# Gated MLP of a two-layer trunk: 16 of 22 up pairs as seven block products, and the down projection in six parts between them

## The chip, the cores and the metric

The kernel runs on one core of one Trainium2 chip. A core has a matrix engine (PE, with its weight loads shown apart as PEld), three engines for elementwise work (DVE, ACT and POOL) and SP, on whose queue nearly all transfers are issued. The metric is the device time of one execution in microseconds; less is better. The program lists each engine's instructions, the engine works through its list in that order, and engines wait for each other by semaphores. So the order of the instructions on an engine is part of the program.

## The reference, cut to what matters

The program computes a decoder trunk of two layers on 512 tokens of width 1024. A layer has a mixer (retention and mLSTM in layer 0, sparse attention in layer 1), a gated MLP with a causal convolution of width 3, and a gated per-layer embedding `e`. The change lies in the MLP and in where `e` is kept:

```
def conv_ffn(h, w_up, conv_w, conv_b, w_down):
    a, b = jnp.split(h @ w_up, 2, axis=-1)
    a = causal_dwconv(a, conv_w, conv_b)
    return (jax.nn.gelu(a) * b) @ w_down
...
        h = h + conv_ffn(rms_norm(h, ffn_norm_g[i]), ffn_w_up[i], ffn_conv_w[i], ffn_conv_b[i], ffn_w_down[i])
        e = rms_norm(p[i] @ ple_w[i], ple_norm_g[i])
        gate = jax.nn.sigmoid(rms_norm(h, ple_gate_norm_g[i]) @ ple_w_gate[i])
```

`w_up` has 2 x 2816 columns and `w_down` 2816 rows, all in float32. A matrix product is made as three products of reduced precision: each operand is split into a rounded high part and a low part (the rest), and high x high, low x high and high x low are summed.

## The kernel before, in words

Activations lie transposed: 128 features on the partitions and the 512 tokens along a row, so that the residual `h` is eight tiles of 128 x 512 (`hp`). The 2816 hidden columns are 22 blocks of 128, numbered f. For each f there is an **up pair**: `mm_up` multiplies the weight columns of the a half and of the b half with the eight normalized activation tiles, 8 x 3 matmuls of 128 x 512 each (`ws`, `mm3`, L162 to L164), into a bank each of PSUM. Both weight tiles come by one DMA of 512 KB each into a `wr` tile; ACT rounds it to the high part `wh` (L134) and DVE subtracts to get the low part `wl` (L135); three sets of these tiles take turns.

`act_up` then makes the hidden block. DVE multiplies the a product by the norm's factor `n.b` (L1326), ACT and two DVE instructions make the convolution (L1329 to L1331), ACT the gelu (L1332), POOL multiplies by `n.b` (L1333), DVE multiplies by the b product (L1334), and the result is split into `gh` (ACT) and `gl` (DVE).

The **down projection** runs in three parts of eight, eight and six f. When the last f of a part is done, `down` goes through the eight output blocks m: one weight tile, 24 or 18 matmuls of 128 x 512, and an addition to `h` by DVE (L1348). A part is one unbroken stretch of PE.

Between the up pairs the embedding `e` of this layer is normed: its squares are summed on ACT and POOL (L218, L220), and POOL multiplies its eight tiles by the norm's factor (L1413). In layer 0 `e` stays in SBUF; in layer 1 it is written to DRAM (tile `emb`) and read back when the MLP begins.

Instructions are issued in the order of the code, except that loads and splits of weights are given a higher priority, so that they move ahead of other work on their engines by up to 500 steps. A tile name is a pool with a fixed number of buffers (`sc`: six scratch tiles, `wr`: three), and an instruction that needs a fresh buffer waits until the last reader of the old one is done.

Of the kernel before, what the change touches and what calls it, by code (L numbers as in the profile page):

```python
# [11 lines left out]
F32 = mybir.dt.float32  # L12
# [15 lines left out]
PARTS = ((0, 8), (8, 16), (16, 22))  # L28
# [13 lines left out]
AHEAD = 500  # L42

# [13 lines left out]
class Norm:  # L57
    def __init__(self):
        self.h, self.l = [], []


class Trunk:
# [83 lines left out]
    def load(self, src, n=1024, cuts=1):  # L146
        nc = self.nc
# [12 lines left out]
    def mm3(self, out, ah, al, bh, bl, first, last):  # L160
        mm = self.nc.tensor.matmul
        mm(out, ah, bh, start=first, stop=False)  # L162
        mm(out, ah, bl, start=False, stop=False)  # L163
        mm(out, al, bh, start=False, stop=last)  # L164
# [46 lines left out]
    def acc_square(self, n, k, src):  # L211
# [4 lines left out]
        else:  # L216
            sq = self.sc()
            nc.scalar.activation(sq, src, AF.Square)  # L218
            eng = nc.vector if k == KD - 1 else nc.gpsimd
            eng.tensor_tensor(n.acc, n.acc, sq, ALU.add)  # L220
# [92 lines left out]
    def ab_mixer(self):  # L313
        nc, I, tc = self.nc, self.I, self.tc
        with ExitStack() as ctx:
# [997 lines left out]
    def ffn(self, i, e):  # L1313
        nc, I, tc = self.nc, self.I, self.tc
        with ExitStack() as ctx:
            fp = ctx.enter_context(tc.tile_pool(name=f"ffn{i}", bufs=1))
            n = self.norm_in(C_FFN + 8 * i)
# [6 lines left out]
            def act_up(f, pa, pb):  # L1324
                a = fp.tile([P, T], F32, name=self.nm("a"), tag="a", bufs=3)
                nc.vector.tensor_tensor(a, pa, n.b, ALU.mult)  # L1326
                c = self.sc()
                cw = C_FCW + 3 * NF * i + 3 * f
                nc.scalar.activation(c, a, AF.Identity, scale=self.col(cw + 2), bias=self.col(C_FCB + NF * i + f))  # L1329
                nc.vector.scalar_tensor_tensor(c[:, 1:], a[:, 0 : T - 1], self.col(cw + 1), c[:, 1:], ALU.mult, ALU.add)  # L1330
                nc.vector.scalar_tensor_tensor(c[:, 2:], a[:, 0 : T - 2], self.col(cw), c[:, 2:], ALU.mult, ALU.add)  # L1331
                nc.scalar.activation(c, c, AF.Gelu_apprx_tanh)  # L1332
                nc.gpsimd.tensor_tensor(c, c, n.b, ALU.mult)  # L1333
                nc.vector.tensor_tensor(c, pb, c, ALU.mult)  # L1334
                hi = fp.tile([P, T], F32R, name=self.nm("gh"), tag="g", bufs=22)
                lo = fp.tile([P, T], F32R, name=self.nm("gl"), tag="g", bufs=22)
                self.split(hi, lo, c)
                gt[f] = (hi, lo)

            def down(part):  # L1340
                f0, f1 = PARTS[part]
                for m in range(KD):
                    hi, lo = self.load(I["w_down"][i, m, :, f0 * P : f1 * P], (f1 - f0) * P)
                    ps = self.bank()
                    for f in range(f0, f1):
                        s = slice((f - f0) * P, (f - f0 + 1) * P)
                        self.mm3(ps, hi[:, s], lo[:, s], gt[f][0], gt[f][1], f == f0, f == f1 - 1)
                    nc.vector.tensor_tensor(self.h[m], self.h[m], ps, ALU.add)  # L1348
# [203 lines left out]
```

## Time and profile before

| | |
|---|---|
| time, median of 3 runs | 1362.65 us (1362.35 to 1362.84) |
| span of the profiled execution | 1361.3 us |
| its granted TensorE clock | 0.999 |
| busy: PE / DVE / ACT / POOL | 1350.9 / 831.5 / 631.1 / 393.3 us |
| share of the span | 99% / 61% / 46% / 29% |

The span goes from the first to the last instruction of one execution; the median of the timed runs lies 1.35 us above it. PE's records overlap, since matmuls are pipelined: the distance from start to start tells the cost of one, not the record's length. The same holds in small for DVE, whose records overlap the next one's start by under 0.1 us when nothing holds them up.

### The profile page before, as it was taken

To read this page: it belongs to the slowest core of one execution; us is meant where nothing else is said; L and a number is where in the kernel's file an instruction comes from. 1 tells how busy PE (TensorE), PEld (TensorE's weight loads), DVE (VectorE), ACT (ScalarE), POOL (GpSimd) and SP (SyncE) were. 2 spreads that over 40 slices of the span, in tenths; PEclk is the share of its full clock that TensorE was granted. 3 is DMA by queue.
4 is the path that set the end of the run, shared out by engine and by line. 5 is a ranking of instruction groups with operands and counts; after the bars stand their busy time and mean duration, and the time that the engine had idled before them with its cause. 6 is when DMAs were issued, how large, how long until landed. Compare 5 with 4: busy or idle time off the path is not lost.

```text
span 1361.3 us, 17932 instructions
## 1 busy us (share of the span) xinstructions
PE 1350.9 (99%) x6702; PEld 1119.9 (82%) x6702; DVE 831.5 (61%) x1296; ACT 631.1 (46%) x1087; POOL 393.3 (29%) x388
## 2 busy tenths in 40 slices
PE   9999999999999999999999999999999999999998
PEld 7888888888888888888788888888888888888887
DVE  6765866565356534557777878766665346435555
ACT  5357526444224313345366888674544133323432
POOL 3356422122032101130421887672122031101120
PEclk9999999999999999999999999999999999999999
DMA  6533333333333332233253221111433333332232
GB/s 221 157 100 93 109 93 108 93 93 102 100 93 93 93 103 96 75 119 121 82 157 117 82 71 52 32 52 54 167 96 105 93 94 95 103 96 89 82 113 74
DMA packets 44096, 135.05 MB, mean 99 GB/s; under 512 B 5348, under 2 KB 5988, under 8 KB 44008
## 3 DMA queue, kind: packets, MB, share of 16 engines
q1 hardware_dynamic: 43720, 133.76, 31.9%
q8 instruction: 53, 0.87, 0.3%
q14 instruction: 35, 0.29, 0.1%
q10 hardware_dynamic: 288, 0.14, 0.0%
HBM read 124.69 MB, written 5.25 MB: 95 GB/s over the span
## 4 chain that ended last, share of the span: by engine, by line
PE 96%; DVE 1%; ACT 1%; POOL 1%; issue 0%; POOLq 0%; ACTq 0%
PE ps L162 28%; PE ps L163 27%; PE ps L164 27%; PE ps L1068 3%; PE ps L1043 2%; PE ps L1012 2%; PE ps L1013 1%; PE ps L392 1%; PE ps L1014 1%; POOL acc L220 1%; PE ps L938 1%; PE ps L961 0%; PE ps L257 0%; PE ps L249 0%; PE ps L460 0%; DVE xf L806 0%
## 5 line engine op out<-in xcount | busy, mean ns | idle before, releaser
L162 PE MATMUL ps<-y,wh 128*128 128x512 f32 (+1 forms) x1112 | 433.1, 391 | 0.9 <-ACT y L134 0.9
L134 ACT ACTIVATE wh<-wr 128x1024 fp32r<-128x1024 f32 (+2 forms) x216 | 223.3, 1036 | 449.4 <-PE ps L163 367.8
L163 PE MATMUL ps<-y,wh 128*128 128x512 f32 (+1 forms) x1112 | 430.8, 388 | 0.0
L164 PE MATMUL ps<-y,wl 128*128 128x512 f32 (+1 forms) x1112 | 429.1, 388 | 0.0
L135 DVE TENSOR_TENSOR wl<-wr,wh 128x1024 fp32r<-128x1024 f32 (+2 forms) x199 | 246.8, 1241 | 93.6 <-ACT wh L134 92.3
L162 PEld LDWEIGHTS ps<-y,wh 128*128 128x128 f32 x1112 | 209.4, 188 | 44.5 <-ACT y L134 1.3
L164 PEld LDWEIGHTS ps<-y,wl 128*128 128x128 f32 x1112 | 208.8, 188 | 42.9
L163 PEld LDWEIGHTS ps<-y,wh 128*128 128x128 f32 x1112 | 209.1, 188 | 41.9
L1333 POOL TENSOR_TENSOR sc<-sc,rb 128x512 f32<-128x512 f32 x44 | 58.8, 1337 | 469.1 <-ACT sc L1332 469.1
L220 POOL TENSOR_TENSOR acc<-acc,sc 128x512 f32<-128x512 f32 x48 | 74.9, 1561 | 238.3 <-ACT sc L218 235.1
L162 PE MATMUL ps<-gh,wh 128*128 128x512 f32 x352 | 136.9, 389 | 0.0
L163 PE MATMUL ps<-gl,wh 128*128 128x512 f32 x352 | 136.6, 389 | 0.0
L164 PE MATMUL ps<-gh,wl 128*128 128x512 f32 x352 | 136.3, 389 | 0.0
L1348 DVE TENSOR_TENSOR hp<-hp,ps 128x512 f32<-128x512 f32 x48 | 33.0, 687 | 128.7 <-PE ps L164 128.7
L1028 POOL TENSOR_SCALAR pr<-pr,sm,gate 128x512 f32<-128x512 f32 (+3 forms) x128 | 76.4, 610 | 29.5 <-DVE sm L1026 24.9
L1326 DVE TENSOR_TENSOR a<-ps,rb 128x512 f32<-128x512 f32 x44 | 30.3, 689 | 84.5 <-PE ps L164 84.5
L163 PEld LDWEIGHTS ps<-gl,wh 128*128 128x128 f32 x352 | 66.1, 188 | 13.7
L162 PEld LDWEIGHTS ps<-gh,wh 128*128 128x128 f32 x352 | 66.1, 188 | 13.7
L164 PEld LDWEIGHTS ps<-gh,wl 128*128 128x128 f32 x352 | 66.1, 188 | 13.7
L1017 ACT ACTIVATE pr<-ps,nmx 128x512 f32<-128x512 f32 (+3 forms) x128 | 68.2, 543 | 14.7 <-DVE nmx L1015 10.2
L1334 DVE TENSOR_TENSOR sc<-ps,sc 128x512 f32<-128x512 f32 x44 | 30.3, 688 | 68.9 <-POOL sc L1333 64.1
L1332 ACT ACTIVATE sc<-sc 128x512 f32<-128x512 f32 x44 | 27.8, 632 | 85.5 <-DVE sc L1331 85.3
(300 smaller groups left out, 2013.6 us busy)
## 6 DMA issues: line engine op xcount, KB each, us to landing
wr<-in_w_up_dram SPq DMA_DIRECT2D x88, 512.0 KB, 3.5
wr<-in_w_down_dram SPq DMA_DIRECT2D x32, 512.0 KB, 3.5
wr<-in_w_plg_dram SPq DMA_DIRECT2D x16, 512.0 KB, 3.6
wr<-in_w_down_dram SPq DMA_DIRECT2D x16, 384.0 KB, 3.1
hp<-in_xT_dram SPq DMA_DIRECT2D x16, 256.0 KB, 4.6
wr<-in_w_abo_dram SPq DMA_DIRECT2D x8, 512.0 KB, 3.7
wr<-in_w_dram SPq DMA_DIRECT2D x8, 512.0 KB, 3.6
wr<-in_w_q_dram SPq DMA_DIRECT2D x8, 512.0 KB, 3.6
```

The costliest lines, as they stand in the source:

```text
L134: self.nc.scalar.activation(hi, src, AF.Copy)
L135: (eng or self.nc.vector).tensor_tensor(lo, src, hi.bitcast(F32), ALU.subtract)
L162: mm(out, ah, bh, start=first, stop=False)
L163: mm(out, ah, bl, start=False, stop=False)
L164: mm(out, al, bh, start=False, stop=last)
L220: eng.tensor_tensor(n.acc, n.acc, sq, ALU.add)
L1017: nc.scalar.activation(pr[:, b], s[:, b], AF.Exp, bias=nmx[:, b : b + 1], accum_out=sm[:, bs[b] : bs[b] + 1])
L1028: nc.gpsimd.tensor_scalar(prs[b], prs[b], sm[:, b : b + 1], gate[:, j, hd, 1 + b : 2 + b], ALU.mult, ALU.mult)
L1068: nc.tensor.matmul(po[0:m, cols], vv[i][:, b, g, 0:m], src, start=False, stop=last and b == 1 and i == 0 and part == 0)
L1326: nc.vector.tensor_tensor(a, pa, n.b, ALU.mult)
L1333: nc.gpsimd.tensor_tensor(c, c, n.b, ALU.mult)
L1348: nc.vector.tensor_tensor(self.h[m], self.h[m], ps, ALU.add)
```

## The change

**Up pairs.** The first six pairs of a layer (`PLAIN = 6`) stay as they were. Pairs 6 to 21 are made as a 2 x 2 x 2 block product with seven instead of eight block products. The blocks are the halves of the 1024 features (four tiles each), the halves of the tokens (256 each) and the two weight columns a and b. A block product is 4 x 3 matmuls of 128 x 256, so a pair is 84 matmuls of 256 columns where it was 48 of 512. Three PSUM banks hold the sums; ACT copies partial sums out of PSUM between products, and DVE adds them.

**Sums of the activations.** `forms`, called after pair 1, makes the sums and differences of activation blocks that the seven products need, with `n.b` folded in: four rounds, each of four DVE instructions of 512 columns that scale or split, two more splits whose low part is left to POOL, and four of 256 on DVE.

**Sums of the weights.** For each of these pairs DVE makes four additions of 512 columns (in `load`, `open` and `rest`) and the low parts of three 1024-wide and one 512-wide tile. `load` brings both weight tiles of a pair.

**Down projection.** Six parts of three or four f. Each part is four jobs of two output blocks m; one job is put after each up pair as soon as its part is complete, and five jobs are left after the last pair. DVE adds to `h` 48 times a layer instead of 24.

**Embedding.** `e` is written to DRAM in both layers, read once for its squares, with the sums on DVE (`early`), and read again after the last pair (`back`); POOL's multiplication by its norm moves into the gate stage (`scaled`).

```diff
-PARTS = ((0, 8), (8, 16), (16, 22))
+PARTS = ((0, 3), (3, 7), (7, 11), (11, 15), (15, 19), (19, 22))
+PLAIN = 6
+H = T // 2
...
+    def forms(self, n, c0):
+        nc = self.nc
+        minus = self.sc()
+        nc.scalar.activation(minus, n.b, AF.Copy, scale=-1.0)
+        sub = lambda out, a, b: nc.vector.tensor_tensor(out, a, b, ALU.subtract)
+        neither = lambda out, a, b: nc.vector.scalar_tensor_tensor(out, a, -1.0, b, ALU.mult, ALU.subtract)
+        n.f = []
+        for k in range(KD // 2):
+            x1, x2 = self.sc(), self.sc()
+            for x, kk in ((x1, k), (x2, k + KD // 2)):
+                nc.vector.scalar_tensor_tensor(x, self.h[kk], self.col(c0 + kk), minus, ALU.mult, ALU.mult)
+            ta, tb = self.sc(), self.sc()
+            b11, b12, b21, b22 = x1[:, :H], x1[:, H:], x2[:, :H], x2[:, H:]
+            sub(ta[:, :H], b11, b12)
+            neither(ta[:, H:], b22, ta[:, :H])
+            sub(tb[:, :H], b22, b12)
+            neither(tb[:, H:], b21, ta[:, H:])
+            one = self.y()
+            self.split(one[:, :H], one[:, H:], b11, nc.gpsimd)
+            got = {1: (one[:, :H], one[:, H:])}
+            for src, left, right in ((x2, 2, 3), (ta, 5, 6), (tb, 7, 4)):
+                hi, lo = self.y(), self.y()
+                self.split(hi, lo, src, nc.gpsimd if left == 2 else nc.vector)
+                got[left], got[right] = (hi[:, :H], lo[:, :H]), (hi[:, H:], lo[:, H:])
+            n.f.append(got)
...
+                def load(me):
+                    f = me.f
+                    me.one = self.wp.tile([P, 1024], F32, name=self.nm("wr"), tag="wr")
+                    me.two = self.slot(f % 4).rearrange("p a t -> p (a t)")
+                    nc.sync.dma_start(me.one, I["w_up"][i, f])
+                    me.s3 = fp.tile([P, T], F32, name=self.nm("es"), tag="es", bufs=2)
+                    nc.sync.dma_start(me.two, I["w_up"][i, NF + f])
+                    nc.vector.tensor_tensor(me.s3, me.one[:, :T], me.two[:, :T], ALU.add)
+                    nc.vector.tensor_tensor(me.two[:, :T], me.two[:, :T], me.two[:, T:], ALU.add)
+
+                def open(me):
+                    me.halves((1, 2), me.one, self.wp, ("wh", "wl"))
+                    nc.vector.tensor_tensor(me.one[:, :T], me.one[:, :T], me.two[:, :T], ALU.add)
+
+                def rest(me):
+                    nc.vector.tensor_tensor(me.one[:, T:], me.one[:, T:], me.one[:, :T], ALU.add)
+                    me.halves((5, 4), me.two, fp, ("fh", "fl"))
+                    me.w[7] = [fp.tile([P, T], F32R, name=self.nm(t), tag=t) for t in ("eh", "el")]
+                    self.split(*me.w[7], me.s3)
+                    me.halves((6, 3), me.one, fp, ("gh", "gl"))
...
+            def product(ps, w, name, first):
+                hi, lo = w[name]
+                for k in range(KD // 2):
+                    s = slice(k * P, k * P + P)
+                    self.mm3(ps, hi[:, s], lo[:, s], *n.f[k][name], first and k == 0, k == KD // 2 - 1, skip_group_check=True)
+
+            def up(f):
+                w = weights(f)
+                one, two, three = [self.ps(t)[:, :H] for t in "aab"]
+                sa, sb = self.sc(), self.sc()
+                copy = lambda out, ps: nc.scalar.activation(out, ps, AF.Copy)
+                a = a_tile()
+                product(one, w, 1, True)
+                copy(sa[:, :H], one)
+                product(two, w, 2, True)
+                nc.vector.tensor_tensor(a[:, :H], two, sa[:, :H], ALU.add)
+                product(one, w, 6, False)
+                copy(sa[:, H:], one)
+                product(three, w, 5, True)
+                copy(sb[:, :H], three)
+                product(one, w, 7, False)
+                copy(sb[:, H:], one)
+                product(three, w, 3, False)
+                nc.vector.tensor_tensor(a[:, H:], three, sa[:, H:], ALU.add)
+                product(one, w, 4, False)
+                nc.vector.tensor_tensor(sb[:, H:], sb[:, H:], sb[:, :H], ALU.add)
+                c = conv(f, a, True)
+                nc.vector.tensor_tensor(c[:, :H], c[:, :H], one, ALU.mult)
+                nc.vector.tensor_tensor(c[:, H:], c[:, H:], sb[:, H:], ALU.mult)
+                keep(f, c)
...
+                if f == 1:
+                    self.forms(n, C_FFN + 8 * i)
+                if jobs:
+                    down(*jobs.pop(0))
+                e.early(f - 1)
+                for part, (f0, f1) in enumerate(PARTS):
+                    if f == f1 - 1:
+                        jobs += [(part, j) for j in range(KD // 2)]
```

The instructions themselves, at three places. A row holds the line of its own kernel, the operation, output and inputs, and the shape; a number after a name tells one tile from another.

**Where `forms` begins.** DVE in layer 0's MLP, from pair 0's last multiplication on, first before and then in the changed kernel. `a`, `sc` and `g` are the tiles of `act_up`, `hp` is `h`, `cols` holds the columns of gains and taps.

```order
L1334 TENSOR_TENSOR sc_2286<-ps_2232,sc_2286 128x512
L1330 SCALAR_TENSOR_TENSOR sc_2361<-a_2359,cols,sc_2361 128x511
L1331 SCALAR_TENSOR_TENSOR sc_2361<-a_2359,cols,sc_2361 128x510
L135 TENSOR_TENSOR gl_2294<-sc_2286,gh_2293 128x512
L1326 TENSOR_TENSOR a_2436<-ps_2380,rb_2277 128x512
L135 TENSOR_TENSOR wl_2485<-wr_2483,wh_2484 128x1024
L1334 TENSOR_TENSOR sc_2361<-ps_2334,sc_2361 128x512
L1330 SCALAR_TENSOR_TENSOR sc_2438<-a_2436,cols,sc_2438 128x511
```

```order
L1389 TENSOR_TENSOR sc_2295<-ps_2241,sc_2295 128x512
L1375 SCALAR_TENSOR_TENSOR sc_2370<-a_2368,cols,sc_2370 128x511
L265 SCALAR_TENSOR_TENSOR sc_2383<-hp_1684,cols,sc_2381 128x512
L265 SCALAR_TENSOR_TENSOR sc_2384<-hp_1687,cols,sc_2381 128x512
L1376 SCALAR_TENSOR_TENSOR sc_2370<-a_2368,cols,sc_2370 128x510
L137 TENSOR_TENSOR g_2303<-sc_2295,g_2302 128x512
L259 TENSOR_TENSOR sc_2387<-sc_2383 128x256
L1386 TENSOR_TENSOR a_2549<-ps_2493,rb_2286 128x512
L137 TENSOR_TENSOR wl_2600<-wr_2598,wh_2599 128x1024
L259 TENSOR_TENSOR sc_2388<-sc_2384,sc_2383 128x256
L260 SCALAR_TENSOR_TENSOR sc_2387<-sc_2384,sc_2387 128x256
L265 SCALAR_TENSOR_TENSOR sc_2408<-hp_1684,cols,sc_2381 128x512
```

Before, pair 2's convolution (on `a_2436`) comes six rows after pair 1's. Now the rows of `forms` (L259, L260, L265) stand behind pair 1's, and the convolution of pair 2 (on `a_2549`) comes 43 rows after pair 1's.

**The first additions to `h`.** DVE in the changed kernel at the end of that stretch. `sc_2551` is pair 2's hidden block, `sc_2631` pair 3's and `sc_2740` pair 4's; `hp_1684` is output block 0.

```order
L1389 TENSOR_TENSOR sc_2551<-ps_2524,sc_2551 128x512
L1376 SCALAR_TENSOR_TENSOR sc_2631<-a_2629,cols,sc_2631 128x510
L137 TENSOR_TENSOR wl_2793<-wr_2785,wh_2792 128x1024
L234 TENSOR_TENSOR acc_2485<-acc_2485,sc_2782 128x512
L1376 SCALAR_TENSOR_TENSOR sc_2740<-a_2738,cols,sc_2740 128x510
L137 TENSOR_TENSOR g_2559<-sc_2551,g_2558 128x512
L1414 TENSOR_TENSOR wr_2785<-wr_2785,ep_2786 128x512
L1389 TENSOR_TENSOR sc_2631<-ps_2604,sc_2631 128x512
L1417 TENSOR_TENSOR wr_2785<-wr_2785 128x512
L1478 TENSOR_TENSOR hp_1684<-hp_1684,ps_2649 128x512
```

Pair 2's low part `g_2559`, on which the first down jobs' last matmuls wait, now stands 60 rows behind pair 1's first convolution instruction, and the first addition to `h` (L1478) 64 rows behind it. Before, no addition to `h` stands in this stretch.

**One stage with a block product pair and a down job.** DVE in the changed kernel, from the low part of a down job's weights to the next pair's multiplications, and PE at the end of a second product and the start of a fifth.

```order
L137 TENSOR_TENSOR wl_4421<-wr_4419,wh_4420 128x1024
L1459 TENSOR_TENSOR a_4148<-ps_4145,sc_4146 128x256
L137 TENSOR_TENSOR gl_4303<-wr_4118,gh_4302 128x1024
L1375 SCALAR_TENSOR_TENSOR sc_4240<-a_4148,cols,sc_4240 128x511
L1451 TENSOR_TENSOR a_4316<-ps_4312,sc_4314 128x256
L1409 TENSOR_TENSOR es_4457<-wr_4454,ep_4455 128x512
L137 TENSOR_TENSOR fl_4295<-ep_4119,fh_4294 128x1024
L1376 SCALAR_TENSOR_TENSOR sc_4240<-a_4148,cols,sc_4240 128x510
L1410 TENSOR_TENSOR ep_4455<-ep_4455 128x512
L137 TENSOR_TENSOR wl_4475<-wr_4454,wh_4474 128x1024
L1463 TENSOR_TENSOR sc_4240<-sc_4240,ps_4143 128x256
L1464 TENSOR_TENSOR sc_4240<-sc_4240,sc_4147 128x256
```

```order
L176 MATMUL ps_2932<-y_2471,wh_2792 128x256
L177 MATMUL ps_2932<-y_2472,wh_2792 128x256
L178 MATMUL ps_2932<-y_2471,wl_2793 128x256
L176 MATMUL ps_2933<-y_2400,fh_2914 128x256
L177 MATMUL ps_2933<-y_2401,fh_2914 128x256
L178 MATMUL ps_2933<-y_2400,fl_2915 128x256
```

The load of the tile `wr_4454` (a later pair's a weights, read by L1409) goes into the buffer that `wr_4419` of the down job gives free, so it is issued after the first row is done. A plain pair has seven DVE instructions (two `wl`, L1386, two of the convolution, L1389, one low part); a block product pair with its job has 19. PE now changes its weights after each 256 columns instead of 512.

More of the change, by code (lines that the diff above doesn't have):

```diff
@@ new lines, in ffn, with weights @@
+            ahead = [Weights(PLAIN)]
+            def weights(f):
+                with tc.high_priority(offset=AHEAD):
+                    now = ahead.pop()
+                    if f + 1 < NF:
+                        ahead.append(Weights(f + 1))
+                        ahead[0].load()
+                    now.rest()
+                    if ahead:
+                        ahead[0].open()
+                return now.w
+            def product(ps, w, name, first):
[3 more added lines that the diff above has]
+                    self.mm3(ps, hi[:, s], lo[:, s], *n.f[k][name], first and k == 0, k == KD // 2 - 1, skip_group_check=True)
@@ L1344, in down @@
+            def down(part, j):
+                f0, f1 = PARTS[part]
+                w = (f1 - f0) * P
+                hi, lo = self.load_parts([I["w_down"][i, m, :, f0 * P : f1 * P] for m in (2 * j, 2 * j + 1)], w)
+                self.cycle = ("b",)
+                for b in range(2):
+                    m = 2 * j + b
                     ps = self.bank()
                     for f in range(f0, f1):
[L1346 removed]
+                        s = slice(b * w + (f - f0) * P, b * w + (f - f0 + 1) * P)
@@ L1361, in ffn @@
-            down(part)
+                if f < PLAIN:
+                    if f == PLAIN - 1:
+                        with tc.high_priority(offset=AHEAD):
+                            ahead[0].load()
+                            ahead[0].open()
+                    act_up(f, *mm_up(f))
+                else:
+                    up(f)
+                if f == 1:
[3 more added lines that the diff above has]
+                e.early(f - 1)
@@ L1362, in ffn, with __init__ @@
+                for part, (f0, f1) in enumerate(PARTS):
+                    if f == f1 - 1:
+                        jobs += [(part, j) for j in range(KD // 2)]
+            e.back()
+            for job in jobs:
+                down(*job)
             self.cycle = ("a",)
     class Embed:
-        def __init__(self, trunk, i, place, away=None):
+        def __init__(self, trunk, i, place, away):
             self.k, self.i, self.place, self.away = trunk, i, place, away
```

116 lines of the change are left out of this document (67 added, 49 removed).

## The prediction

> **What bounds the kernel now.** I read the page's shares first, then the chain of waits, then the matrix engine's start times.
>
> ```profile
> span 1361.3 us, 17932 instructions
> PE 1350.9 (99%) x6702; PEld 1119.9 (82%) x6702; DVE 831.5 (61%) x1296; ACT 631.1 (46%) x1087; POOL 393.3 (29%) x388
> PE 96%; DVE 1%; ACT 1%; POOL 1%; issue 0%; POOLq 0%; ACTq 0%
> DVE hp L1348 <- PE ps L164: 128.7, 46, 5.0
> ```
>
> PE is busy for all but 10 us, and 96% of the chain that ended last is PE. DVE's additions to `h` wait for PE, not the other way. So PE time taken away is gained in full, as long as no other engine becomes late; and any wait that PE gets is lost in full. The change does both kinds of thing: fewer columns through PE, more work on DVE.
>
> **Term 1: the products.** A pair was 48 matmuls of 512 columns and becomes 84 of 256, for 16 pairs in each of two layers. The last stretch of the run holds both widths with nothing between them:
>
> ```profile
> 1334.82 0.39 PE L163 MATMUL ps<-y,wh 128*128 128x512 f32 x1
> ...
> 1350.68 0.39 PE L164 MATMUL ps<-y,wl 128*128 128x512 f32 x1
> 1350.91 0.28 PE L162 MATMUL ps<-y,wh 128*128 128x256 f32 x1
> ...
> 1356.54 0.28 PE L164 MATMUL ps<-y,wl 128*128 128x256 f32 x1
> ```
>
> From the first to the second row are 70 steps: 15.86 / 70 = 0.2266 us for 512 columns. From the third to the fourth are 47: 5.63 / 47 = 0.1198 us for 256, which is 53% and not half. Each of these has its own weight load in both cases. A pair goes from 48 x 0.2266 = 10.88 us to 84 x 0.1198 = 10.06 us, so seven products instead of eight save not an eighth but 7.5%: 0.81 us. Over 32 pairs: **-26.0 us**. If 256 columns cost just half (0.1133 us), it would be 32 x 1.36 = 43.5 us; that is the upper bound.
>
> The Trainium skill, "TensorE: Matmul & The Clock Gate", section "Back-to-back issue gap", lists 518 cycles for 512 columns and 262 for 256; by that ratio (0.506) term 1 would be an estimated 40 us. The trace's 0.1198 us disagrees, and I take the trace.
>
> **Term 2: a stage in which a block product pair meets a down job.** PE needs 10.06 us and 24 matmuls of 512, 5.44 us: 15.5 us. DVE's 19 instructions there, by start to start:
>
> ```profile
> 1160.16 1.22 DVE L135 TENSOR_TENSOR wl<-wr,wh 128x1024 fp32r<-128x1024 f32 x1
> 1161.30 0.68 DVE L135 TENSOR_TENSOR gl<-sc,gh 128x512 fp32r<-128x512 f32 x1
> ...
> 227.88 0.75 DVE L231 SCALAR_TENSOR_TENSOR y<-hp,cols,y 128x512 fp32r<-128x512 f32 x1
> 228.55 0.68 DVE L306 TENSOR_TENSOR hp<-hp,ps 128x512 f32<-128x512 f32 x1
> ...
> 264.13 0.73 DVE L1330 SCALAR_TENSOR_TENSOR sc<-a,cols,sc 128x511 f32<-128x511 f32 x1
> 264.90 0.75 DVE L1331 SCALAR_TENSOR_TENSOR sc<-a,cols,sc 128x510 f32<-128x510 f32 x1
> 265.57 0.68 DVE L135 TENSOR_TENSOR gl<-sc,gh 128x512 fp32r<-128x512 f32 x1
> 266.18 0.68 DVE L1326 TENSOR_TENSOR a<-ps,rb 128x512 f32<-128x512 f32 x1
> L1295 DVE TENSOR_TENSOR pt<-ps,pt 128x256 fp32r<-128x256 f32 x16 | 6.7, 419 | 4.3 <-ACT pt L1046 4.3
> wr<-in_w_up_dram SPq DMA_DIRECT2D x88, 512.0 KB, 3.5
> y<-emb SPq DMA_DIRECT2D x8, 256.0 KB, 5.0
> L134 ACT ACTIVATE wh<-wr 128x1024 fp32r<-128x1024 f32 x196 | 207.2, 1059 | 415.0 <-PE ps L163 344.1 <-issue 32.9 <-PE ps L164 19.8
> L1329 ACT ACTIVATE sc<-a,cols 128x512 f32<-128x512 f32 x44 | 35.5, 808 | 4.2 <-DVE a L1326 3.9
> L1332 ACT ACTIVATE sc<-sc 128x512 f32<-128x512 f32 x44 | 27.8, 632 | 85.5 <-DVE sc L1331 85.3
> L1046 ACT ACTIVATE pt<-ps 128x256 fp32r<-128x256 f32 x16 | 6.5, 408 | 4.5 <-PE ps L1043 4.5
> ```
>
> 1024 columns take 1.14 us, a scalar-tensor-tensor of 512 0.67, one of the convolution 0.77, a plain 512 0.61 (I use 0.62). For 256 there is only a record of 0.419; as the 512 record stands 0.07 above its step, I use 0.38. The stage: 4 x 1.14 + 8 x 0.62 + 5 x 0.38 + 2 x 0.77 = 13.0 us, 84% of 15.5. DVE also closes a loop there with a transfer: the low part of the down weights frees the buffer, the next weights land 3.5 us later, and L1409 behind it waits for them. From that low part to L1409 the loop takes 3.7 us with its signals; then 15 instructions, L1409 the first, run until the next such low part is done: 10.4 us by the steps above. That makes 14.1 us, 1.4 under PE. So I cost the stage at **0**, covered by PE. The loop's upper end: records (10.4 becomes 11.2) and a transfer as slow as `emb`'s 5.0 us give 16.4 us, 0.9 us over PE.
>
> The jobs with three f in a part bring PE's share to 14.1 us, level with the loop. In the stages up to f = 9 the squares of `e` and one norm cost DVE some 3 us more in all; the 16% it has free takes them. The 48 additions to `h` are among the 19. ACT has four copies of 256, four splits of 1024, the convolution's start, the gelu and two splits of 512: 4 x 0.41 + 4 x 1.06 + 0.81 + 3 x 0.63 = 8.6 us of 15.5. The transfers of `e` (8 more writes in layer 0, 16 reads a layer) are short beside the weights on SP's queue, and POOL's multiplications in the gate stage (8 of 1.34 us by L1333's row below) lie beside PE's 8 x 24 matmuls of 5.4 us: all at 0; uncovered they would be 8 x 1.34 = 10.7 us a layer.
>
> **Term 3: the stretch from `forms` to the first additions to `h`.** Here I find no cover. DVE stands in line 64 instructions deep between pair 1's first convolution and the first addition to `h`, and PE's last matmuls of the first down jobs wait for `g_2559` and then, for their bank, for that addition. The 64: 5 of 1024 (5.7 us), 2 of 768 (0.88 by the record below less 0.07: 1.8), 8 scale instructions of `forms` (8 x 0.67 = 5.4), 16 of 256 (16 x 0.38 = 6.1), 8 of the convolution (8 x 0.77 = 6.2), 25 of 512 (25 x 0.62 = 15.5): 40.6 us.
>
> ```profile
> L135 DVE TENSOR_TENSOR wl<-wr,wh 128x768 fp32r<-128x768 f32 x16 | 15.3, 955 | 0.1
> 259.88 0.69 DVE L1326 TENSOR_TENSOR a<-ps,rb 128x512 f32<-128x512 f32 x1 [0.73 <-PE ps L164]
> ```
>
> The clock of this starts when PE ends pair 1's a product, just before 259.88; pair 1's first convolution instruction began at 264.13, 4.25 us later, and nothing ahead of it changes. So the first addition to `h` ends at 4.25 + 40.6 + 0.7 = 45.6 us. PE has until then pairs 2, 3 and 4 and 27 matmuls of down jobs: 171 x 0.2266 = 38.8 us. DVE is late by **6.8 us in each layer**, if nothing slows it down.
>
> But POOL works in this stretch too, and then DVE is slowed:
>
> ```profile
> 289.10 0.74 DVE L1330 SCALAR_TENSOR_TENSOR sc<-a,cols,sc 128x511 f32<-128x511 f32 x1
> 289.29 1.69 POOL L220 TENSOR_TENSOR acc<-acc,sc 128x512 f32<-128x512 f32 x1 [6.54 <-ACT sc L218]
> 289.88 1.66 DVE L1331 SCALAR_TENSOR_TENSOR sc<-a,cols,sc 128x510 f32<-128x510 f32 x1
> L1331 DVE SCALAR_TENSOR_TENSOR sc<-a,cols,sc 128x510 f32<-128x510 f32 x44 | 43.9, 997 | 1.4
> L1326 DVE TENSOR_TENSOR a<-ps,rb 128x512 f32<-128x512 f32 x44 | 30.3, 689 | 84.5 <-PE ps L164 84.5
> L1333 POOL TENSOR_TENSOR sc<-sc,rb 128x512 f32<-128x512 f32 x44 | 58.8, 1337 | 469.1 <-ACT sc L1332 469.1
> L931 POOL TENSOR_TENSOR y<-ep,y 128x256 fp32r<-128x256 f32 x8 | 5.6, 733 | 0.0
> ```
>
> L1331 takes 0.75 us alone and 1.66 beside POOL's addition: 0.91 us lost, and its mean over the kernel is 997 ns. L1326, which reads one operand from PSUM, has a mean of 689 and never shows it. Before, this cost nothing, as DVE had 39% to spare; in this stretch it has nothing. POOL's instructions there are the low parts of `forms` (4 of 512, 4 of 256) and three multiplications by `n.b`: 7 x 0.95 + 4 x 0.45 (733 ns less the same 0.3 us of overlap) = 8.4 us, of which a tenth falls on PSUM readers: 7.6 us. The range: 0, if POOL's work falls into DVE's waits, to the whole of POOL's time, 7 x 1.34 + 4 x 0.73 = 12.3. I take 7.6, since the queue leaves DVE hardly a wait. Together 6.8 + 7.6 = 14.4 us a layer; layer 1 has the same order. Term 3: **+28.8 us**, from 13.6 to 38.
>
> The Trainium skill, "SBUF — State Buffer", section "Who interferes with whom", says that a DVE instruction with two SBUF inputs and a POOL instruction that reads SBUF exclude each other; the rows above agree, and by it all of POOL's 12.3 us would stand against DVE, 38 us for term 3.
>
> **Sum.** 1361.3 - 26.0 + 0 + 28.8 = 1364.1 us of span, and 1.35 more for the median of runs (1362.65 against 1361.3): **1365.5 us**. The saving and the new stall cancel; a stall of 13.0 us a layer is where they do.
>
> **Rivals.**
>
> *The stall is small.* POOL's instructions hit DVE's waits, or DVE gets ahead of my list: 6.8 us a layer, 1361.3 - 26.0 + 13.6 + 1.35 = 1350.3 us. For it: several of the rows in the stretch wait for ACT, so DVE has holes that POOL may use. Against: 1.66 us rows come even where DVE is half idle. Chance 0.22.
>
> *The stages run at DVE's pace.* Place: the loop of down weights, transfer and L1409. Price: at 16.4 us instead of 15.5, 0.9 us on each of some 28 stages, 25 us: 1390 us, slower. It decides from 1.4 us of delay in the loop on. For it: 3.5 us is a median with one or two transfers at a time, and in-order DVE rows wait on ACT, which waits on PE. Against: the pair's other weights have a buffer of their own and land a stage ahead, and DVE is only 84% full. Chance 0.15.
>
> *256 columns cost half.* The array streams half the columns in half of 0.2266 us, and the end of the run is slowed by something else: 43.5 us saved, with the stall 1348 us. The 47 even steps speak against it; 0.05. The table of the Trainium skill cited above would have it nearly so.
>
> *The change does not do what it says.* The order shows 84 matmuls of 256 in each such pair, so only a clock below 0.999 could undo it; 0.03, about 1375 us.
>
> **How the numbers follow.** My forecast, stall of 11 to 18 us a layer and stages at PE's pace, has 0.55: by itself 1359 to 1373 us. A measurement of this kernel tells 0.2% (2.7 us) from no change: faster ends at 1359.9, slower begins at 1365.4. Of my 0.55, 0.05 is faster, 0.23 the same and 0.27 slower. With the rivals: faster 0.05 + 0.22 + 0.05 = 0.32, same 0.23, slower 0.27 + 0.15 + 0.03 = 0.45. The range for 8 in 10 goes from 1347 (small stall, a little less than its 6.8 us) to 1382 (a third to a half of the loop's price on top of the forecast).
>
> **What would show it.** Term 1: starts 0.12 us apart in the 256-column rows, 10.1 us a pair. Term 2: PE without gaps from f = 7 on, 15.5 us from job to job, and L1409 with a wait of about 1 us for its transfer. Term 3: one gap of PE in each layer, ahead of the first matmuls that read `g_2559` and the bank of the first L1478, of 14 us in all, with DVE over 95% busy for 50 us before it, and DVE rows of 1.6 us beside POOL's. The prediction is wrong if PE's idle time in that stretch is under 10 us a layer or if gaps recur in each stage.

## The result, and the profile after

The changed kernel takes **1376.7 us** (median of 4 runs, 1375.1 to 1377.2) against 1362.6 us before, run beside it: ratio 1.0101, 95% interval 1.0089 to 1.0113. It is slower by 1.0%. The forecast was 1365.5 us, the range 1347 to 1382; slower by over 0.2% had the largest chance, 0.45.

The page of the profiled execution, its shares and its chain of waits:

```profile
span 1375.3 us, 20999 instructions
PE 1338.8 (97%) x7854; PEld 1157.2 (84%) x7854; DVE 1054.0 (77%) x1708; ACT 736.0 (54%) x1313; POOL 365.3 (27%) x360
PE 85%; DVE 8%; ACT 3%; issue 2%; POOL 1%; DMA 1%; DVEq 0%; POOLq 0%; ACTq 0%
PEclk9999999989999999999999999999989999999999
```

PE is busy 12 us less than before, but the span is 14 us longer: PE's idle time grew from 10.4 to 36.5 us. The chain, 96% PE before, now has 8% DVE and 3% ACT in it. And the clock row has an 8 in slice 9 and slice 30, the MLP of layer 0 and of layer 1.

The stretch of `forms` on PE, in the timeline of the changed kernel (start, length, and in brackets the idle time and what ended it):

```profile
285.31 0.50 PE L178 MATMUL ps<-g,wl 128*128 128x512 f32 x1 [0.52 <-DVE wl L137]
...
295.64 0.39 PE L178 MATMUL ps<-g,wl 128*128 128x512 f32 x1
298.62 0.47 PE L176 MATMUL ps<-g,wh 128*128 128x512 f32 x1 [2.59 <-ACT sc L1374]
298.93 0.40 PE L177 MATMUL ps<-g,wh 128*128 128x512 f32 x1
300.60 0.50 PE L178 MATMUL ps<-g,wl 128*128 128x512 f32 x1 [1.27 <-DVE wl L137]
...
305.42 1.65 PE L176 MATMUL ps<-g,wh 128*128 128x512 f32 x3 [3.13 <-ACT g L136]
309.43 0.80 PE L177 MATMUL ps<-g,wh 128*128 128x512 f32 x1 [2.36 <-DVE g L137]
310.02 0.63 PE L178 MATMUL ps<-g,wl 128*128 128x512 f32 x1
310.45 0.63 PE L177 MATMUL ps<-g,wh 128*128 128x512 f32 x1
...
314.62 0.44 PE L178 MATMUL ps<-g,wl 128*128 128x512 f32 x1
...
321.50 0.28 PE L176 MATMUL ps<-y,wh 128*128 128x256 f32 x1
```

The five waits add up to 9.9 us. The last is where the prediction put it, ahead of the low part of pair 2's hidden block (`g`, 309.43); the others are for what stands ahead of it in DVE's and ACT's lists. The matmuls between and behind them start up to 0.43 us apart instead of 0.227. The prediction's second condition, the first addition to `h`, is in the row of PE's weight loads:

```profile
312.32 0.29 PEld L176 LDWEIGHTS ps<-g,wh 128*128 128x128 f32 x1 [0.69 <-DVE hp L1478]
```

So up to 312.32 us it is still DVE that sets the pace, also of the slow matmuls. What DVE and POOL do meanwhile:

```profile
282.94 2.31 DVE L137 TENSOR_TENSOR wl<-wr,wh 128x1024 fp32r<-128x1024 f32 x1
289.23 5.96 POOL L137 TENSOR_TENSOR y<-sc,y 128x256 fp32r<-128x256 f32 x2 [5.06 <-ACT y L136]
293.97 0.72 ACT L1374 ACTIVATE sc<-a,cols 128x512 f32<-128x512 f32 x1 [3.39 <-POOL y L137]
294.73 1.01 DVE L1375 SCALAR_TENSOR_TENSOR sc<-a,cols,sc 128x511 f32<-128x511 f32 x1 [1.39 <-ACT sc L1374]
```

DVE's split of 1024 columns, 1.14 us by itself, takes 2.31 us beside POOL; two low parts on POOL take 5.96 us; ACT waits 3.39 us for them before it can start pair 2's convolution, since they hold the scratch tile that it needs, and DVE then waits 1.39 us for ACT.

The clock, from the view of the changed kernel by windows (stretch, length, then busy time of PE, PEld, DVE, ACT and POOL with the number of instructions, the granted clock, DMA share and GB/s):

```profile
300.00:302.00 2.00, 1.40 (x4) 0.82 (x4) 2.00 (x2) 2.00 (x3) 1.69 (x1) 0.77 0.20 30
304.00:306.00 2.00, 0.58 (x1) 0.50 (x2) 2.00 (x4) 1.59 (x3) 0.00 (x0) 0.50 0.04 14
312.00:314.00 2.00, 2.00 (x5) 1.39 (x5) 2.00 (x4) 1.11 (x2) 0.00 (x0) 0.50 0.20 80
316.00:318.00 2.00, 2.00 (x10) 1.64 (x10) 2.00 (x3) 0.62 (x1) 0.00 (x0) 1.00 0.78 259
```

The clock is granted at half from 301.1 to 314.7 us. PE is fully busy from 310 on, and the window from 312 still shows only five matmuls, where the one from 316 shows ten.

Behind the stretch PE is gapless for long (140 us from 420 to 560 without idle time), but not everywhere. At pair 9:

```profile
375.33 0.33 SPq L1406 DMA_DIRECT2D wr<-in_w_up_dram  x1
375.71 0.42 SPq L1549 DMA_DIRECT2D sc<-emb  x1
379.23 1.06 ACT L136 ACTIVATE wh<-wr 128x1024 fp32r<-128x1024 f32 x1 [0.28 <-DMA wr<-in_w_up_dram]
379.96 0.28 PE L177 MATMUL ps<-y,fh 128*128 128x256 f32 x1
380.19 0.71 ACT L1374 ACTIVATE sc<-a,cols 128x512 f32<-128x512 f32 x1
380.80 1.04 ACT L136 ACTIVATE fh<-ep 128x1024 fp32r<-128x1024 f32 x1
381.89 0.39 PE L176 MATMUL ps<-y,fh 128*128 128x256 f32 x1 [1.53 <-ACT fh L136]
```

The next pair's weights land 3.9 us after their issue, a load of `e` for its squares beside them. ACT's rounding of these weights (`wh`) stands in its queue ahead of the convolution and of `fh`, which PE is waiting for. ACT itself waits for the transfer only 0.28 us here. And `fh` has one buffer, which PE's last product of the old pair reads until the row at 379.96: ACT could not have begun the new `fh` before about 380.25, so at most 0.55 us of the 1.53 are due to ACT's queue, and the rest is the rounding itself, which PE has nothing else to cover with.

### The profile page after: what moved, and what is told of

Read it like the earlier page. It is cut to its first block, busy times and chain, and to the rows that moved or that the text cites. A ratio compares the mean times of both kernels' runs of the same rounds, so it can differ in the third digit from the quotient of the medians.

```text
span 1375.3 us, 20999 instructions
## 1 busy us (share of the span) xinstructions
PE 1338.8 (97%) x7854; PEld 1157.2 (84%) x7854; DVE 1054.0 (77%) x1708; ACT 736.0 (54%) x1313; POOL 365.3 (27%) x360
## 4 chain that ended last, share of the span: by engine, by line
PE 85%; DVE 8%; ACT 3%; issue 2%; POOL 1%; DMA 1%; DVEq 0%; POOLq 0%; ACTq 0%
PE ps L176 24%; PE ps L177 24%; PE ps L178 23%; PE ps L1108 3%; PE ps L1083 2%; DVE wl L137 2%; PE ps L1052 1%; PE ps L1053 1%; ACT wh L136 1%; POOL y L137 1%; PE ps L432 1%; DVE sc L1376 1%; PE ps L1054 1%; POOL acc L234 1%; DMA wr<-in_w_up_dram 1%
## 5 line engine op out<-in xcount | busy, mean ns | idle before, releaser
L176 PE MATMUL ps<-y,wh 128*128 128x512 f32 (+1 forms) x664 | 230.9, 351 | 0.9 <-ACT y L136 0.9
L177 PE MATMUL ps<-y,wh 128*128 128x512 f32 (+1 forms) x664 | 229.2, 347 | 0.0
L178 PE MATMUL ps<-y,wl 128*128 128x512 f32 (+1 forms) x664 | 228.0, 346 | 0.0
L176 PE MATMUL ps<-g,wh 128*128 128x512 f32 x544 | 214.3, 398 | 11.3 <-ACT g L136 6.1
L177 PE MATMUL ps<-g,wh 128*128 128x512 f32 x544 | 215.2, 396 | 4.7 <-DVE g L137 4.7
L178 PE MATMUL ps<-g,wl 128*128 128x512 f32 x544 | 214.7, 395 | 3.6 <-DVE wl L137 3.6
L176 PEld LDWEIGHTS ps<-y,wh 128*128 128x128 f32 x664 | 126.0, 190 | 19.0 <-ACT y L136 1.3
L177 PEld LDWEIGHTS ps<-y,wh 128*128 128x128 f32 x664 | 125.8, 189 | 16.0
L178 PEld LDWEIGHTS ps<-y,wl 128*128 128x128 f32 x664 | 125.6, 189 | 15.7
L176 PEld LDWEIGHTS ps<-g,wh 128*128 128x128 f32 x544 | 103.2, 191 | 34.1 <-ACT g L136 7.5
L178 PEld LDWEIGHTS ps<-g,wl 128*128 128x128 f32 x544 | 104.0, 191 | 26.6 <-DVE wl L137 5.3
L177 PEld LDWEIGHTS ps<-g,wh 128*128 128x128 f32 x544 | 103.9, 191 | 25.2 <-DVE g L137 6.2
L176 PE MATMUL ps<-y,fh 128*128 128x256 f32 x256 | 73.0, 285 | 5.0 <-ACT fh L136 5.0
L1478 DVE TENSOR_TENSOR hp<-hp,ps 128x512 f32<-128x512 f32 x96 | 65.0, 680 | 16.7 <-PE ps L178 16.5
L178 PE MATMUL ps<-y,gl 128*128 128x256 f32 x256 | 72.5, 283 | 0.0
```

The source lines that it names most:

```text
L176: mm(out, ah, bh, start=first, stop=False, **kw)
L177: mm(out, ah, bl, start=False, stop=False, **kw)
L178: mm(out, al, bh, start=False, stop=last, **kw)
```

## The experiments

All times are medians; "before" was run again beside each group of runs (1362.2 to 1362.7 us). The changed kernel of 1376.7 us is what each is held against.

### Three quarters of forms left out (x1)

```diff
         for k in range(KD // 2):
+            if k:
+                n.f.append(n.f[0])
+                continue
             x1, x2 = self.sc(), self.sc()
```

> Leaves out three of the four rounds of forms (the sums of round 0 stand in for all; every matmul and every other instruction stays). Theory A (PE's loss of 15.0 us a layer in the forms stretch is DVE's queue there, 64 instructions plus what POOL adds): DVE has 12.3 us less to do by its own instructions and about 4 us less beside POOL, so the stall all but goes: 1376.7 - 2 x 15 = 1347 us, 1343 to 1352. Theory B (the stall hangs on where the first down jobs stand, not on how much DVE does ahead of them): 1370 us or more. Theory C (the stages at DVE's pace cost most of it): at most 10 us less, 1367 us or more.

**1348.6 us**, ratio to before 0.9898 (0.9883 to 0.9912): theory A, to 2 us. PE's order is the same in both, so the first 256-column matmul tells the stretch's price. In this run:

```profile
306.11 0.28 PE L176 MATMUL ps<-y,wh 128*128 128x256 f32 x1
```

306.11 against 321.50: 15.4 us in layer 0, of which 0.3 is there before the MLP begins (its first matmul starts at 236.24 and 236.51 us), so 15.1; by the same count it is 15.0 in layer 1. The window from 262 to 320 us, this run first and then the changed kernel:

```profile
262.00:320.00 58.00, 58.00 (x277) 48.82 (x276) 52.18 (x70) 30.42 (x43) 11.66 (x8) 1.00 0.47 152
```

```profile
262.00:320.00 58.00, 48.12 (x191) 37.15 (x190) 54.52 (x74) 28.23 (x44) 23.24 (x13) 0.88 0.30 99
```

277 matmuls in 58 us at a clock of 1.00 (those behind 306 us partly of 256 columns), and 191 at 0.88.

### forms' low parts from POOL to DVE (x2)

```diff
-            self.split(one[:, :H], one[:, H:], b11, nc.gpsimd)
+            self.split(one[:, :H], one[:, H:], b11, nc.vector)
...
-                self.split(hi, lo, src, nc.gpsimd if left == 2 else nc.vector)
+                self.split(hi, lo, src, nc.vector)
```

> The low parts that forms leaves to POOL (4 of 512, 4 of 256 columns a layer) go to DVE, all else as in the change. Theory A (POOL's instructions cost a full DVE nearly their own time): DVE gains 4 x 0.95 + 4 x 0.45 = 5.6 us a layer and pays 4 x 0.62 + 4 x 0.38 = 4.0, and ACT no longer waits for POOL's last low part (3.4 us once, 1.4 of it passed on to DVE): 1.6 to 3 us less a layer, 1371 to 1374 us. Rival (POOL's work is free for DVE): 4.0 us more a layer, 1384.7 us.

**1376.7 us** (ratio to before 1.0104, 1.0089 to 1.0119): neither. DVE has eight more instructions a layer (4.0 us by the prediction's steps) and is not later; so POOL's eight cost it about as much as doing them itself, and the rival that they are free falls. The gain of 1.6 to 3 us a layer isn't there either.

### The down projection in six parts alone (x4)

```diff
-PLAIN = 6
+PLAIN = 22
...
-                if f == 1:
-                    self.forms(n, C_FFN + 8 * i)
...
-                return fp.tile([P, T], F32R, name=self.nm("g"), tag="g", bufs=22)
+                return fp.tile([P, T], F32R, name=self.nm("g"), tag="g", bufs=34)
```

> All 22 pairs plain, no forms, no block products: only the down projection in six parts between the pairs, the embedding's detour and the moved multiplication are left of the change (the pool of hidden tiles has 34 buffers instead of 22, since without the block products the activations stay in it). Theory A: PE has the matmuls of before, and DVE's 24 more additions a layer (15 us) hide: 1362.6 us, 1360 to 1366. Rival (the jobs between the pairs, or POOL's multiplications beside the gate, make waits of their own): 1368 us or more, and then that share of the change's +14.1 us is theirs.

**1363.1 us**, ratio 1.0004 (0.9995 to 1.0014): no change. The order of the down jobs, the 48 additions more and the embedding's detour cost nothing by themselves, in a kernel whose DVE has neither `forms` nor the weight sums to do.

### forms spread over pairs 1 to 4 (x5)

```diff
-        for k in range(KD // 2):
+        for k in ks:
...
-                if f == 1:
-                    self.forms(n, C_FFN + 8 * i)
+                if 1 <= f <= 4:
+                    self.forms(n, C_FFN + 8 * i, (f - 1,))
```

> The four rounds of forms one by one after pairs 1, 2, 3 and 4 instead of all after pair 1; ACT makes its -n.b tile four times (0.6 us each). Same work on every engine but for that. Theory A: until pair 5 PE has 5 x 10.9 + 3 x 4.1 = 66.6 us, DVE by the steps some 73 us with POOL's hold-ups, so about 7 us of stall a layer are left of 15: 1361 us, 1352 to 1367. Rival (DVE's total until pair 6 sets it and the order does not matter): 1374 us or more.

**1366.2 us**, ratio 1.0029 (1.0018 to 1.0041): 10.5 us less than the change, and inside the expected range though 5 us above its centre. The order of the same work on DVE is worth that much.

### The squares of e after pairs 10 to 18 (x3)

```diff
-                e.early(f - 1)
+                e.early(f - 10)
```

> The squares of e and their norm come after pairs 10 to 18 instead of 1 to 9. In the change PE lost 15.0 us a layer in the forms stretch and some 5 us more behind it, of which 1.9 (pair 9, waiting for fh), 0.5 and 0.9 us (norm of e) fall where the squares and the norm of e run beside the block products. Theory A (three of the 64 instructions ahead of the first addition are these squares, 0.62 us each; the later losses come from squares and norm too): 1.9 us less in the stretch and up to 3 us less behind it a layer, if the norm costs nothing later either: 1367 to 1373 us. Rival (the later losses belong to the stages themselves, and the norm's wait just moves): only the stretch's share, 1372 to 1375.

**1377.8 us**, ratio 1.0113 (1.0096 to 1.0130): no gain, against theory A. The stretch got 1 to 2 us shorter, and the loss came back where the squares now stand, pair by pair, for instance at pair 14:

```profile
457.48 0.38 PE L176 MATMUL ps<-y,gh 128*128 128x256 f32 x1 [1.14 <-ACT sc L1446]
```

### Four edits together (x6)

Spread, low parts on DVE, late squares, and:

```diff
-                nc.gpsimd.tensor_tensor(c, c, n.b, ALU.mult)
+                nc.vector.tensor_tensor(c, c, n.b, ALU.mult)
```

> Four edits together: forms spread over pairs 1 to 4, its low parts on DVE, the plain pairs' multiplication by n.b on DVE (so POOL has nothing to do there), and the squares of e after pairs 10 to 18. Theory A: DVE's excess until pair 5 shrinks by 0.95 - 0.62 us for each of 5 multiplications, by some 0.6 us for the low parts and 2.5 us for four squares, from x5's 9.8 us of loss to about 4; with no gap over 2.5 us the clock stays up: 1366 - 2 x 5 to 6 = 1355 us, 1350 to 1360. Rival (the wait only goes to the next instruction in DVE's queue, now the weight splits that PE needs): 1363 us or more.

**1354.1 us**, ratio 0.9942 (0.9927 to 0.9957): faster than before, as theory A had it. The stretch has no gap left, but PE loses time beside the squares, more than in the change (8.7 us in layer 0 behind the stretch instead of 4.2). ACT, SP and PE of this run at one of these places:

```profile
420.63 0.33 SPq L1406 DMA_DIRECT2D wr<-in_w_up_dram  x1
421.06 0.44 SPq L1551 DMA_DIRECT2D sc<-emb  x1
425.07 1.06 ACT L136 ACTIVATE wh<-wr 128x1024 fp32r<-128x1024 f32 x1 [2.37 <-DMA wr<-in_w_up_dram]
426.04 0.61 ACT L136 ACTIVATE eh<-es 128x512 fp32r<-128x512 f32 x1
426.56 0.36 ACT L1446 ACTIVATE sc<-ps 128x256 f32<-128x256 f32 x1
426.98 0.38 PE L176 MATMUL ps<-y,fh 128*128 128x256 f32 x1 [1.55 <-ACT sc L1446]
```

The weights take 4.4 us to land with the load of `e` behind them, ACT stands 2.37 us in front of them, and the copy out of PSUM that PE needs stands behind in ACT's queue. PE waits 1.55 us.

### e read back behind the last jobs (x7)

```diff
-            e.back()
             for job in jobs:
                 down(*job)
+            e.back()
```

> e is read back behind the last down jobs instead of ahead of them, so that POOL's multiplications cannot start beside the last block product. Theory A (the 1.0 us gap of PE at the last pair comes from three POOL multiplications that hold up DVE there): that gap goes, 1.2 us less a layer, unless the gate now waits for e: 1374.3 us, 1373 to 1376. Rival (the gap is the stage's own): 1376 to 1378.

**1376.0 us**, ratio 1.0099 (1.0084 to 1.0114): no difference from the change that the spread of the runs (1375.1 to 1376.8) lets see. The edit did not move what it was meant to move: the first four reads of `e` are still issued between 553 and 556 us, and POOL's multiplications run as far ahead of the gap as they do in the change. So this run decides for neither theory.

```profile
559.32 4.43 POOL L1556 TENSOR_TENSOR y<-y,rb 128x512 f32<-128x512 f32 x3 [1.91 <-DMA y<-emb]
569.20 0.39 PE L176 MATMUL ps<-y,fh 128*128 128x256 f32 x1 [1.03 <-ACT fh L136]
```

What the gap waits for can be read from the rows of the change, where it ends at 570.59:

```profile
569.48 1.06 ACT L136 ACTIVATE fh<-ep 128x1024 fp32r<-128x1024 f32 x1 [0.38 <-PE ps L177]
```

ACT was idle and waited for PE's last reading of the old `fh` (a matmul at 569.16), rounded the new one in 1.06 us, and PE needs it at once. Neither DVE nor POOL is in this chain. x1, x10 and x11 have the same gap of 1.03 us at their last pair.

### Matmuls to fill the stall (x8)

```diff
+                        if part == 0 and j == 0 and b == 0 and f == f1 - 1:
+                            pw = self.ps("o")
+                            for _ in range(40):
+                                nc.tensor.matmul(pw, lo[:, 0:P], gt[f0][0], start=True, stop=True)
```

> 40 matmuls more a layer (9.1 us at full clock) into an unused bank, ahead of pair 4's products, so that PE is busy in most of the time in which it otherwise waits for DVE; they feed nothing. Theory A (in the change the granted clock falls to 0.50 some 5 us after PE's first gap and makes 12 to 18 matmuls behind the stall 0.2 us longer each): the stall is filled, the clock stays near 1.00, and 2.5 us a layer are saved: 1371.5 us, 1369 to 1374. Rival (the clock is no part of the loss): 1376.7 us; and if the matmuls come on top: up to 1395.

**1375.7 us**, ratio 1.0097 (1.0082 to 1.0112): 1.0 us less instead of 5, and within the spread of the change's runs. The 80 matmuls did fit into the stall, but a gap of 2.75 us was left. In layer 0, some 5 us after it began, the clock went to half for 3.4 us, in which PE was busy. This gap, and the clock by windows of 2 us:

```profile
303.52 0.73 PE L176 MATMUL ps<-g,wh 128*128 128x512 f32 x2 [2.75 <-ACT g L136]
```

```profile
304.00:306.00 2.00, 1.74 (x8) 1.07 (x7) 2.00 (x3) 0.21 (x1) 0.38 (x1) 0.89 0.00 0
306.00:308.00 2.00, 2.00 (x6) 1.61 (x5) 1.96 (x4) 1.24 (x2) 0.00 (x0) 0.50 0.07 8
308.00:310.00 2.00, 2.00 (x8) 1.54 (x8) 2.00 (x4) 1.46 (x2) 0.66 (x1) 0.76 0.75 248
```

In layer 1 of the same execution the same gap (2.75 us, up to 1023.38) left the clock at 1.00:

```profile
1020.00:1030.00 10.00, 7.00 (x30) 5.15 (x29) 9.15 (x12) 4.83 (x9) 2.86 (x3) 1.00 0.27 78
```

The stretch was only 0.5 us shorter than the change's there too, but a wait of 1.64 us for a weight's low part has come into it, so what the clock alone costs isn't measured apart. The rows of the change bound it: behind 312.32 us, where DVE no longer sets the pace, the slow matmuls lose 1.2 us in layer 0 and 1.1 in layer 1.

### Where the squares of e stand (x9, x10 and x11)

Three more, the first two on top of the four edits. Squares after every second pair:

```diff
-                e.early(f - 10)
+                if f >= 6 and f % 2 == 0:
+                    e.early((f - 6) // 2)
+                if f == NF - 1:
+                    e.early(KD)
```

> As x6 (forms spread, its low parts and the n.b multiplications on DVE), but the squares of e after every second pair, 6 to 20, and their norm after the last. In x6 the stretch of forms costs PE nothing any more (0.3 us), and 9 us a layer go in pairs 13 to 18, beside squares in every stage and the norm. Theory D (a stage with a square, its load and its norm is about 1 us over PE's 15.5 and one without about 1.4 us under it, so squares in a row add up and squares apart do not): 9 us become 2 to 4, 1354.1 - 2 x 6 = 1342 us, 1339 to 1347. Rival (each square costs its wait wherever it stands): 1352 to 1356.

**1351.3 us**, ratio 0.9917 (0.9902 to 0.9931): 2.8 us better than x6, nearer to the rival. Theory D's picture of slack that a stage without a square gives back is not borne out.

Squares back after pairs 1 to 9, so only three edits are left:

```diff
-                e.early(f - 10)
+                e.early(f - 1)
```

> As x6, but the squares of e after pairs 1 to 9, where the change has them. Theory D: four squares and their loads come back into the stretch of forms (2.5 us of DVE, 0 to 3 us of PE), and behind it some 4.8 us are lost as in the change instead of 9: 1354.1 - 2 x 1 to 4 = 1349 us, 1346 to 1353. Rival (the squares in the stretch bring the stall back): 1358 or more.

**1344.8 us**, ratio **0.9870** (0.9855 to 0.9885): 1.3% faster than before and 2.3% faster than the change, better than expected. The same 120 us in the middle of the MLP, x6 first and then this kernel:

```profile
420.00:540.00 120.00, 113.89 (x797) 106.02 (x796) 95.70 (x154) 60.71 (x95) 0.00 (x0) 1.00 0.32 102
```

```profile
420.00:540.00 120.00, 119.53 (x837) 111.97 (x835) 96.80 (x146) 61.62 (x94) 1.93 (x1) 1.00 0.29 93
```

40 matmuls more, and PE 5.6 us busier, now that no squares stand in these stages. And the early stretch of this kernel:

```profile
262.00:320.00 58.00, 57.88 (x274) 48.34 (x273) 58.00 (x95) 35.03 (x54) 0.00 (x0) 1.00 0.38 116
```

DVE is busy without a pause and does 95 instructions where the change did 74 in 54.5 us; POOL does nothing.

The change itself without six of the eight squares:

```diff
-                e.early(f - 1)
+                if f in (1, 2, 9):
+                    e.early(f - 1)
```

> The change with six of the eight squares of e left out (those after pairs 3 to 8; those after 1 and 2 and the norm after 9 stay), so that e's norm is too small. Theory D: the 2.4 us a layer that PE loses at pair 9 ahead of the norm go, and 1.2 us of the forms stretch with two additions: 1376.7 - 2 x 3.6 = 1369.5 us, 1367 to 1372. Rival (the loss at pair 9 belongs to the first 15.5 us stages behind the stretch): only the stretch's share, 1373 to 1375.

**1372.5 us**, ratio 1.0073 (1.0057 to 1.0090): 4.2 us less, a little more than the rival's share and less than theory D's. Behind the stretch PE is 2.1 us faster in layer 0 and 1.8 in layer 1; the change and this run from 360 to 420 us:

```profile
360.00:420.00 60.00, 57.93 (x408) 54.12 (x407) 51.25 (x87) 31.39 (x48) 0.00 (x0) 1.00 0.35 115
```

```profile
360.00:420.00 60.00, 60.00 (x416) 56.02 (x415) 47.82 (x72) 30.03 (x48) 0.00 (x0) 1.00 0.33 105
```

PE has no gap there any more. But leaving out the squares also changed the order of the instructions: at pair 9 ACT's rounding of `fh` (376.05) now stands ahead of that of the next weights (378.48), and on PE 34 matmuls of other products lie between the last reading of the old `fh` and the first of the new. So the squares cause the gap, but by way of the order as much as by their own work; this run does not part the two. What gave less than expected was the stretch of `forms`: the first 256-column matmul of layer 0 starts at 319.47 instead of 321.50 us, 0.6 of which is there when the MLP begins, and in layer 1 the stretch is no shorter than in the change.

### Which of POOL's two tasks (x12)

The kernel of 1344.8 us with forms' low parts on POOL again:

```diff
-            self.split(one[:, :H], one[:, H:], b11, nc.vector)
+            self.split(one[:, :H], one[:, H:], b11, nc.gpsimd)
...
-                self.split(hi, lo, src, nc.vector)
+                self.split(hi, lo, src, nc.gpsimd if left == 2 else nc.vector)
```

> As x10, but forms' low parts are left on POOL again: forms spread over pairs 1 to 4, and the plain pairs' multiplication by n.b on DVE. Spreading alone gave 1366.2 us, spreading with both edits 1344.8, and the low parts alone, without spreading, nothing. Theory E (the multiplication by n.b is what costs: on POOL it stands in a chain from gelu to the hidden block that PE waits for, behind low parts that a full DVE keeps from running): 1347 us, 1344 to 1352. Rival F (forms' low parts on POOL cost it, as they hold scratch tiles that the next round of forms waits for): 1358 us or more. In between: both.

**1354.6 us**, ratio 0.9941 (0.9925 to 0.9958): in between, so both. From spread alone (1366.2), moving the multiplication to DVE gives 11.6 us, moving the low parts too another 9.8.

## Why the prediction was right or wrong

**Term 1, the products: right.** 256-column matmuls start 0.12 us apart in the changed kernel's block products too (340.16 to 341.48 us: 11 steps, 1.32 us), and the six-parts kernel shows that nothing else of the change takes PE time. -26.0 us stands.

**Term 3, the stretch of forms: right in place, cause and size, wrong in part of its make-up.** Forecast 14.4 us a layer, shown 15.1 and 15.0 by the run that leaves three rounds out (its whole time is only 28.1 us less, since it loses some 2 us again behind the stretch). The queue of 64 instructions is the cause: less work in it (x1) or another order of it (x5) shortens the stall, while the six-part order alone costs nothing. DVE was busy for 54.5 of 58 us, 94% where I had said 95. From pair 1's first convolution (264.14) to the first addition to `h` (311.59) DVE takes 47.5 us, where the sum said 40.6 + 7.6 = 48.2. But I had forecast one gap of 14 us; it is 9.9 us in five pieces, and between and behind them matmuls run at a granted clock of 0.50. No term had that. The 11 steps from 309.43 to 314.62 take 5.19 us, 2.7 more than at 0.2266; what comes ahead of 312.32 is hidden behind DVE, so the clock adds 1.2 us to the stretch.

**POOL in that stretch: the price right, the mechanism half.** I priced what POOL costs DVE at 7.6 us. In the rows of layer 0 ten DVE instructions beside POOL's are longer than the prediction's steps, by 7.0 us in all. Exchanging eight of POOL's instructions for 4.0 us of DVE work left the time the same, so their part, 5.6 us, was somewhat high. What I did not price is what DVE costs POOL. The groups of the changed kernel:

```profile
L137 POOL TENSOR_TENSOR y<-sc,y 128x256 fp32r<-128x256 f32 x8 | 20.0, 2494 | 29.0 <-ACT y L136 29.0
```

A low part of 256 columns takes 2494 ns on average, where one of this shape took 733 before. The average hides two cases: the four of layer 0 take 0.75, 3.71, 0.82 and 4.71 us. POOL's results come late, and scratch tiles with them. The rule of the Trainium skill that the prediction cited ("SBUF — State Buffer", "Who interferes with whom") has the exclusion go both ways; these rows agree, and I used one way of it. They show more than that sentence: 3.71 us is longer than POOL's own 0.75 and the longest DVE split (1.14 us alone) together, so POOL is held up by more than one DVE instruction. With the spread order this is worth 21.4 us for the kernel (1366.2 to 1344.8), far over what DVE's own time explains: 13 POOL instructions at 0.95 and 0.45 us against 9 x 0.62 + 4 x 0.38 = 7.1 us of DVE come to 3.3 us a layer. Which part of the rest is late results and which the clock isn't separated.

**Term 2, the stages: the failed step.** "So I cost the stage at **0**, covered by PE", and for the squares "the 16% it has free takes them". The first half held for most stages: from 420 to 560 us, nine of them, PE has no gap, and L1409's wait for its transfer is there (12 waits, 9.3 us, where I had said about 1 us each). But term 2 measures at about +10 us instead of 0: the span's +14.0 is -26.0 + 30.1 + the rest, 9.9. Counted from start to start in layer 0, PE's three waits behind the stretch cost 1.69 us at pair 9, 0.70 at the norm of `e` and 1.19 at the last pair; the matmuls right behind them lose 0.6, and some 100 steps of up to 0.03 us another 0.8.

I counted DVE's load, and DVE has room. ACT I priced by its sum, 8.6 of 15.5 us, and did not ask which buffer it waits for and what is queued behind a wait. Where PE's list puts the last product that reads the old `fh` right ahead of the first that reads the new one, ACT's rounding into the only buffer lies open: 1.03 us at the last pair, beside no square, and the larger part of the 1.53 at pair 9. The rest there is ACT's order, the next pair's weights and a convolution ahead of `fh`. Where squares follow one another (x6), a transfer that is late holds up ACT with a copy behind it that PE needs, 1.55 us.

**The rivals.** The small stall is refuted by x1. The stage at DVE's pace is refuted as put (no 0.9 us a stage); a loop through a transfer does cost in x6's stages with squares, but through ACT. Half cost for 256 columns is refuted by the starts. By the ratio in the table of the Trainium skill that the prediction cited ("TensorE: Matmul & The Clock Gate", "Back-to-back issue gap") they would be an estimated 0.115 us apart; the rows have 0.12.

**The sum.** 1365.5 us was 11.2 us short: some 10 us from the stages, and 1.3 from the stretch, where the clock, which I had left out, adds 2.3 and the rest came out a little shorter than my sum. That the time still lies in the range is partly luck: the room above the forecast was meant for a loop at DVE's pace, and what filled it were three waits a layer for ACT and the norm.

## What to carry to other kernels

When PE work is cut at the price of work on an engine that is two thirds busy, walk that engine's queue from the first new instruction to the first one that PE waits for: the mean share says nothing, the 64 instructions did. Do the same for every engine that waits for a transfer or for a buffer, and price what stands behind the wait, not only the engine's sum. Work that is needed late should be issued a piece at a time between what is needed soon, and where DVE is full nothing should be left on POOL: with these two the same block products turned +1.0% into -1.3%.

## What the runs showed of the hardware that was not expected

The granted clock follows PE's gaps with a delay, and the length of one gap doesn't settle it. Gaps of 1.53 us (the change, up to 381.89) and 1.55 us (x6) left it at 1.00. One of 2.57 us (x12, up to 303.98) brought 0.50 from 304.4 us on, 3.0 us after it began; one of 2.75 us (x8) did so after 4.8 us in layer 0 and not at all in layer 1. Four gaps of 1.27 to 3.13 us within 13.4 us (the change) brought it 5.0 us after the first began, and PE was busy again for 5.3 us before it ended. In layer 0 the stretches at 0.50 last 3.41 us (x8, x12), 6.83 (x5), 10.24 (x3, x11) and 13.65 (the change, x2, x7): multiples of 3.41. So a stall of PE can be paid a second time, in matmuls that wait for nothing; in the change that was 1.2 of 15.1 us.

DVE and POOL hold each other up, and beside a full DVE it is POOL that comes off worse: of its 256-column subtractions in the stretch two took 3.71 and 4.71 us instead of 0.73, over several DVE instructions each, while ten DVE instructions together lost 7.0 us.
